# All later conditioning products as two fp16 parts with one constant scale, loaded singly through two buffers, and five raw places for the streamed weights

## The chip, the cores and the metric

The kernel runs on one core of one Trainium2 chip. The metric is the device time of one execution in microseconds. The core has five engines that run side by side: PE (TensorE, the matrix unit), DVE (VectorE), ACT (ScalarE), POOL (GpSimd) and SP (SyncE, which only issues transfers). ACT and POOL can issue transfers too. Each engine and each issuing queue takes its own instructions in a fixed order.

## The reference

One inference step of a one-layer decoder trunk for 288 tokens: a prompt of 256 tokens and 8 sequences of 4 tokens. The model width is 2048. The weights and all inputs are float32.

```python
mod = jax.nn.silu(c) @ P['w_ada'] + P['b_ada']
sh1, sc1, gt1, sh2, sc2, gt2 = [m[:, None, :] for m in jnp.split(mod, 6, axis=-1)]
xn = rmsnorm(x, P['g_norm1']) * (1.0 + sc1) + sh1
mix, st = mixer(xn, states[l], P)
x = x + gt1 * mix
xn = rmsnorm(x, P['g_norm2']) * (1.0 + sc2) + sh2
x = x + gt2 * (jnp.square(jax.nn.relu(xn @ P['w_ff1'])) @ P['w_ff2'])
...
y = rmsnorm(x, g_final)
```

`c` has 9 rows: one for the prompt and one for each of the 8 sequences. So the conditioning product `silu(c) @ w_ada` reads a matrix of 2048 x 12288 for only 9 rows; it gives the shift, scale and gate of both norms. `mixer` multiplies `xn` with `w_in`, runs three branches (a gated linear recurrence, gated linear attention "GLA", and mLSTM with a matrix memory), multiplies each branch with a weight of its own, merges the three products with sigmoid gates, and multiplies with `w_out`. The feed-forward has width 8192. The outputs are `y` and the new states of all branches.

## The kernel before

All activations lie with features on the 128 partitions and the 288 tokens along the row. The kernel holds two versions of the program: a fast one, and a full one in float32 that runs only where a flag, computed at the end of the fast one, says that its scaling was out of range. `fast` in the code tells them apart. Only the fast one runs here.

**Large weights.** `stream` (its matmuls are line 211 of the profile) goes through a block of 512 output columns in granules. For each granule it loads 128 x 1024 float32 values (512 KB) from memory into a raw place, has ACT write the high part (`hi`, scaled by a constant, line 198) and DVE the rest (`lo`, line 134, with a sum of the rest as a mark in the tile `gd`), both fp16, and then has PE do 24 matmuls of 288 columns: hi times x's high part, hi times x's low part, lo times x's high part. A block over 2048 features has 8 granules, one over 1024 has 4. The pairs of parts lie in five buffers. The raw places are three tiles of their own (`raw`) and four quarters of the tile `xl`, used in a ring of seven. From the output projection on, only the three tiles are used.

**Order.** The instructions of SP stay in the order in which the program is traced (`tc.manual_schedule` for SP). Those of the other engines are ordered when the program is built, by priorities and a simulated timeline, and then stay fixed. `Q` is SP's queue, `G` is POOL's, `S` is ACT's. Inside the feed-forward (`in_order`) PE, ACT and DVE keep the traced order too; its matmuls are line 275 and its conversions line 184.

**Stages.** Early blocks (48 granules, while the scale and shift of the first norm are computed), GLA's gate (16), first merge (48), mLSTM input (16), second merge (48), mLSTM output gate (16), third merge (48), output projection (32), feed-forward (252 steps). A merge takes four times 8 granules for a gate and 4 for a branch. The three branches run beside the merges, a step after each granule (`beside`, `run`).

**Conditioning.** The parts of `w_ada` for GT1, SH2, SC2 and GT2 (the gate of the mixer's residual, the second norm's shift and scale, and the gate of the feed-forward's residual) come in 64 units of 1 MB: 16 for GT1 (two halves of 1024 columns each) and eight for each half of the other three (`sj0`, `sj1` for SH2, `sm0`, `sm1` for SC2, `gt0`, `gt1` for GT2). A unit is loaded, held in the list `held`, and later visited: its small matmuls go to one bank `pa`, 32 columns wide, four groups side by side. `every` sets a pattern of letters, and after each granule `run` does the next one: L loads the next unit (`load_one`; the buffer is the next of `slots["ids"]`, the queue is `slots["queue"]`), V visits all units held, F up to four, C does one step of a unit's conversion, E evaluates a result put off, a point does nothing. A load must wait until the last reader of its buffer is done.

Two kinds of units exist before. `cond_product` multiplies the float32 weights directly (line 390). `cond_parts` (line 451), used for `sj1`, `sm1` and `gt1`, first finds a scale for each row from the sum of absolute values (ACT, line 429; DVE, lines 430 to 432), then writes the high part (ACT, line 435) and the rest (DVE, line 437, into every second half word of the raw buffer itself), and scales the 32 columns of `silu(c)`, which lie as three bf16 parts (`silu_parts`), for that row.

From the mLSTM output gate on, the loads go out on SP:

```python
merge(1, ygla, io["wbg"])
slots.update(ids=(None,), n=0, queue=Q)
every("L . . CC CC V" + 12 * " .", skip=10)
...
visit()
slots.update(ids=(None, "st", 5), n=0)
every("L L . L CC CC CC CC CC CC . V . . . L L L CC CC CC CC CC CC V" + 3 * " . . . L L L V", skip=4)
merge(2, yml, io["wbm"])
```

`None` stands for the tile `ag`, which the second merge also uses for its gates; `"st"` for a pair of tiles, and a number for one of ten large tiles.

**Second norm.** After the last output projection block come the residual, the sum of squares, the root (`rstd_of`), `second_norm` and the first feed-forward matmuls. The units of `gt0` are visited in that stretch.

**Check.** `certify` squares the marks in `gd`, sums them over the partitions with one matmul (line 140), and reduces them to one number (lines 139 to 143); it is called twice early in the feed-forward and twice near its end.

Of the kernel before, what the change touches and what calls it, by code (L numbers as in the profile page):

```python
# [8 lines left out]
F32 = mybir.dt.float32  # L9
# [45 lines left out]
def trunk(ctx, tc, io, fast):  # L55
    nc = tc.nc
    R = F16 if fast else F32R
    WS, XS, YS, MS, ZS = (2.0 ** e if fast else 1.0 for e in (14, 6, 5, 4, 4))
# [61 lines left out]
    gd = wp.tile([P, 768], F32, tag="gd", name="gd", bufs=1) if fast else None  # L120
    marks = [0, 544]

    def mark(w=False):

        if not fast:
            return None
        i = 0 if w else 1
        marks[i] += 1
        assert marks[0] <= 544 and marks[1] <= 768
        return gd[:, marks[i] - 1:marks[i]]  # L130
# [5 lines left out]
    def certify(of, a, b, least):  # L136

        sq, p = t288()[:, 0:b - a], misc()[:, 0:b - a]
        V.tensor_tensor(out=sq, in0=gd[:, a:b], in1=gd[:, a:b], op=ALU.mult)
        T.matmul(p, ones, sq, start=True, stop=True)  # L140
        V.tensor_scalar(sq, p, least, None, ALU.is_ge)
        V.scalar_tensor_tensor(sq, p, BIG, sq, ALU.is_le, ALU.mult)
        V.tensor_reduce(out=of, in_=sq, axis=AX.X, op=ALU.min)
# [211 lines left out]
    def raw_tile():  # L355
# [5 lines left out]
        if i in ("xh", "xl"):  # L361
# [47 lines left out]
    high = {"ids": (None,), "n": 0}  # L409

    def high_tile():

        i = high["ids"][high["n"] % len(high["ids"])]
        high["n"] += 1
        if i is None:
            return sp.tile([P, 2048], F16, tag="uh", name=nm("uh"), bufs=3)
        if "xl" not in high:
            high["xl"] = flat(big.tile([P, KT, N], F32, tag="xl", name=nm("xl")))[:, 0:4096].bitcast(F16)
        return high["xl"][:, 2048 * i:2048 * i + 2048]

    def cond_parts(name, load, each, finish):
# [3 lines left out]
        def parts(u, ks):  # L425

            e = [[sc([P, 1], "ue", 12) for _ in range(2)] for _ in u]
            for (w, h, c), (t, scale) in zip(u, e):
                S.activation(h, w, AF.Abs, accum_out=t)
                V.tensor_scalar(t.bitcast(I32), t.bitcast(I32), 0x7F800000, None, ALU.bitwise_and)  # L430
                V.tensor_scalar(t, t, 2.0 ** -86, 2.0 ** -14, ALU.max, ALU.mult)
                V.tensor_scalar(scale.bitcast(I32), t.bitcast(I32), -1, 254 << 23, ALU.mult, ALU.add)
                yield
            for (w, h, c), (t, scale), k in zip(u, e, ks):
                S.activation(h, w, AF.Copy, scale=scale)
                S.activation(c, silp[:, 32 * k:32 * k + 32], AF.Copy, scale=t)
                V.scalar_tensor_tensor(words(w, 0, F16), w, scale, h, ALU.mult, ALU.subtract)  # L437
                yield

        def products(u, q):  # L440
# [3 lines left out]
            for _ in u[1]:  # L444
                pass
            for i, (w, h, c) in enumerate(u[0]):
                a = 0 if each == 2 else 256 * i
                for n, v in enumerate((h, words(w, 0, F16))):
                    v = v.rearrange("p (m j f) -> p j m f", j=4, f=32)
                    for j in range(4):  # L450
                        pace["prod"] = T.matmul(ps[32 * j:32 * j + 32, a:a + 256], c, v[:, j], start=q == i == n == 0,
                                                stop=q == KT // each - 1 and n == 1, skip_group_check=True)

        def end():
            for h in range(3 - each):
                with tc.high_priority():
# [3 lines left out]
                    V.tensor_tensor(out=pv[:, :, 0:9], in0=pv[:, :, 0:9], in1=o, op=ALU.add)  # L460
                    finish(h, pv)

        for q in range(KT // each):
            def ld(q=q):
                raw = raw_tile()
                load(raw, q)
                w = raw if len(raw) == 2 else [raw[0][:, 0:1024], raw[0][:, 1024:2048]]
                h = high_tile()
                u = [(w[i], h[:, 1024 * i:1024 * i + 1024], sp.tile([P, 32], BF16, tag="uc", name=nm("uc"), bufs=6)) for i in range(2)]
                return u, parts(u, [each * q + (i if each == 2 else 0) for i in range(2)])  # L470
# [19 lines left out]
    def ada(kind):  # L490
        def load(raw, k):
# [3 lines left out]
            else:  # L495
                slots["queue"].dma_start(raw[0].rearrange("p (h m) -> p h m", h=2), wada[kind][:, k].rearrange("h p m -> p h m"))
        return cond_product(kind, load, 1, 2048, silu_c, ada_finish(kind))

    def ada_half(name, kind, h, parts=False):
# [6 lines left out]
        if parts:  # L506
# [40 lines left out]
    def units():  # L547
# [8 lines left out]
        for h in range(2):  # L556
            yield from ada_half(f"sj{h}", SH2, h, h == 1)
        for h in range(2):
            yield from ada_half(f"sm{h}", SC2, h, h == 1)
        for h in range(2):  # L560
            yield from ada_half(f"gt{h}", GT2, h, h == 1)
# [15 lines left out]
    def visit(n=99):  # L577

        evaluate()
        for _ in range(min(n, len(held))):  # L580
            name, raw, products, end = held.pop(0)
            products(raw)
            if end:
                done.add(name)
                if name == "gt0":
# [4 lines left out]
    def step(cs):  # L590
        for c in cs:
# [4 lines left out]
            elif c == "C":  # L596
                with tc.issue_after(pace["hi"].ins), tc.issue_after(pace["lo"].ins):
                    next((0 for u in held if len(u[1]) == 2 and next(u[1][1], 1) is None), 0)
# [79 lines left out]
    if fast:  # L678
# [3 lines left out]
        at.update(raw=(None, 0, None, 1, None, 2, 3))  # L682
# [282 lines left out]
    every("")  # L965
    slots.update(queue=G)
# [32 lines left out]
    every("L L L L V . . .")  # L999
    slots.update(ids=(6, 7, "st", None), n=0)  # L1000
# [328 lines left out]
    def merge(br, y, w):  # L1329
        for b in range(4):  # L1330
            if br == 0 and b == 2:
                visit()
                slots.update(ids=(None,), n=0)
                every("L . V . . .", skip=5)
# [12 lines left out]
            if br == 1 and b == 0:  # L1347
                finish(gla_[0])
                slots.update(ids=("st",), n=0)
# [783 lines left out]
```

## Time and profile before

| what | value |
| --- | --- |
| median of 3 runs | 1841.35 us (1841.3 to 1843.49) |
| profiled execution | 1841.84 us, span of its instructions 1840.0 us |
| PE busy | 1778.8 us, 97% of the span |
| DVE, ACT, POOL busy | 1159.8, 931.1, 209.5 us |
| moved by DMA | 422.98 MB, mean 230 GB/s |
| mean granted clock of PE | 0.991 |

The span runs from the first to the last instruction of the program; the rest of the execution's time lies around it. An engine is busy while one of its instructions runs; issuing a transfer or waiting is not counted. In rows of groups stand the line, the engine, the operation, what is written and read, the shapes and the count, then busy time, mean duration in ns, and the idle time of the engine just before these instructions with what ended it. In a timeline a row has its start, its length, and in brackets the idle time ahead of it and what ended that.

### The profile page before, as it was taken

To read this page: it belongs to the slowest core of one execution; us is meant where nothing else is said; L and a number is where in the kernel's file an instruction comes from. 1 tells how busy PE (TensorE), PEld (TensorE's weight loads), DVE (VectorE), ACT (ScalarE), POOL (GpSimd) and SP (SyncE) were. 2 spreads that over 40 slices of the span, in tenths; PEclk is the share of its full clock that TensorE was granted. 3 is DMA by queue.
4 is the path that set the end of the run, shared out by engine and by line. 5 is a ranking of instruction groups with operands and counts; after the bars stand their busy time and mean duration, and the time that the engine had idled before them with its cause. 6 is when DMAs were issued, how large, how long until landed. Compare 5 with 4: busy or idle time off the path is not lost.

```text
span 1840.0 us, 38642 instructions
## 1 busy us (share of the span) xinstructions
PE 1778.8 (97%) x15784; PEld 1380.0 (75%) x15784; DVE 1159.8 (63%) x2575; ACT 931.1 (51%) x1364; POOL 209.5 (11%) x287
## 2 busy tenths in 40 slices
PE   8999999999999999999999999999999999999996
PEld 6787667786777877777767677777777777777775
DVE  4778855646684467886459676556666655555565
ACT  5324475445455354576359465645545544444443
POOL 0002201111142010011002510000000000000261
PEclk9999999999999999999999999999999999999998
DMA  9999756647845469656797775566565555555531
GB/s 394 414 409 355 275 213 246 218 161 286 277 149 173 141 202 316 228 207 251 278 362 293 285 279 170 183 217 206 176 211 186 186 172 183 175 181 180 176 127 54
DMA packets 113451, 422.98 MB, mean 230 GB/s; under 512 B 11808, under 2 KB 12096, under 8 KB 110064
## 3 DMA queue, kind: packets, MB, share of 16 engines
q1 hardware_dynamic: 97040, 361.04, 55.7%
q0 software_dynamic: 11472, 42.79, 6.6%
q10 hardware_dynamic: 4752, 16.60, 2.3%
q8 instruction: 125, 2.05, 0.5%
q14 instruction: 62, 0.51, 0.1%
HBM read 403.56 MB, written 16.81 MB: 228 GB/s over the span
## 4 chain that ended last, share of the span: by engine, by line
PE 56%; DMA 5%; DVE 5%; ACT 2%; issue 2%; SPq 0%; POOL 0%; ACTq 0%; DVEq 0%; POOLq 0%
PE mm L275 32%; PE mm L211 12%; PE pi L275 8%; DMA raw<-wout 2%; DVE pair L134 2%; ACT pair L198 1%; DMA xl<-wbm 1%; PE pa L390 1%; DMA st<-mC 1%; DMA xl<-win 1%; DVE s L437 0%; DMA s<-mC 0%; PE px L1597 0%; DMA o_C_s<-st 0%; PE px L1683 0%
## 5 line engine op out<-in xcount | busy, mean ns | idle before, releaser
L211 PEld LDWEIGHTS <-pair 128*128 128x128 f16 x6528 | 631.3, 98 | 210.1 <-issue 23.2
L275 PEld LDWEIGHTS <-pair 128*128 128x128 f16 x6144 | 601.8, 98 | 159.8 <-issue 5.5
L211 PE MATMUL mm<-x,pair 128*128 128x288 f16 x4320 | 562.0, 288 | 6.6 <-DVE s L769 2.2
L134 DVE SCALAR_TENSOR_TENSOR pair<-xl,pair 128x1024 f16<-128x1024 f32 x229 | 282.9, 1238 | 219.9 <-ACT pair L198 117.0
L134 DVE SCALAR_TENSOR_TENSOR pair<-raw,pair 128x1024 f16<-128x1024 f32 x207 | 255.4, 1235 | 196.6 <-ACT pair L198 116.6
L275 PE MATMUL mm<-hx,pair 128*128 128x288 f16 x2472 | 320.2, 287 | 0.0
L275 PE MATMUL mm<-z,pair 128*128 128x288 f16 x2448 | 313.1, 288 | 4.0 <-ACT z L1854 3.4
L211 PE MATMUL mm<-s,pair 128*128 128x288 f16 x1920 | 245.9, 288 | 11.1 <-ACT ag L1341 3.6
L198 ACT ACTIVATE pair<-xl 128x1024 f16<-128x1024 f32 x137 | 144.0, 1054 | 201.8 <-PE mm L211 121.2
L198 ACT ACTIVATE pair<-raw 128x1024 f16<-128x1024 f32 x135 | 142.0, 1052 | 159.2 <-PE mm L211 77.5
L134 DVE SCALAR_TENSOR_TENSOR pair<-s,pair 128x1024 f16<-128x1024 f32 x92 | 113.8, 1237 | 104.4 <-ACT pair L184 104.4
L184 ACT ACTIVATE pair<-s 128x1024 f16<-128x1024 f32 x92 | 96.9, 1054 | 120.9 <-PE mm L275 99.7
L184 ACT ACTIVATE pair<-xl 128x1024 f16<-128x1024 f32 x92 | 96.8, 1055 | 120.9 <-PE mm L275 94.4
L184 ACT ACTIVATE pair<-raw 128x1024 f16<-128x1024 f32 x72 | 75.7, 1054 | 97.5 <-PE mm L275 70.6
L1879 POOL TENSOR_SCALAR s<-s,mod 128x256 f32<-128x256 f32 x16 | 14.7, 921 | 665.1 <-DVE s L1895 665.1
L275 PE MATMUL pi<-hx,pair 128*128 128x288 f16 x600 | 89.9, 287 | 0.0
L275 PE MATMUL pi<-z,pair 128*128 128x288 f16 x624 | 85.6, 288 | 0.0
L211 PE MATMUL px<-x,pair 128*128 128x288 f16 x288 | 41.8, 287 | 3.4 <-DVE pair L134 2.8
L1364 POOL TENSOR_TENSOR s<-s,t 128x288 f32<-128x288 f32 x16 | 20.0, 1279 | 162.7 <-DVE t L1363 130.9
L390 PE MATMUL pa<-s,silc 128*32 128x128 f32 (+2 forms) x768 | 33.0, 320 | 1.7 <-DVE silc L317 1.2
L134 DVE SCALAR_TENSOR_TENSOR hx<-t,hx 128x288 f16<-128x288 f32 x64 | 29.3, 458 | 6.7
L1873 DVE TENSOR_TENSOR t<-t 128x288 f32<-128x288 f32 x64 | 29.2, 456 | 3.0
(494 smaller groups left out, 1544.3 us busy)
## 6 DMA issues: line engine op xcount, KB each, us to landing
xl<-win SPq DMA_DIRECT2D x109, 512.0 KB, 5.5
s<-wf SPq DMA_DIRECT2D x92, 512.0 KB, 3.4
xl<-wf SPq DMA_DIRECT2D x92, 512.0 KB, 3.5
raw<-win SPq DMA_DIRECT2D x83, 512.0 KB, 6.1
raw<-wf SPq DMA_DIRECT2D x72, 512.0 KB, 3.4
s<-wq SPq DMA_DIRECT2D x20, 1024.0 KB, 13.0
raw<-wout SPq DMA_DIRECT2D x32, 512.0 KB, 6.5
s<-wada SPq DMA_DIRECT2D x13, 1024.0 KB, 8.3
```

The costliest lines, as they stand in the source:

```text
L134: return V.scalar_tensor_tensor(dst, src, scale, hi if fast else hi.bitcast(F32), op, ALU.subtract, accum_out=mark(w))
L184: pace["hi"] = S.activation(hi, raw, AF.Copy, scale=WS)
L198: pace["hi"] = S.activation(hi, raw, AF.Copy, scale=WS)
L211: pace["last"] = T.matmul(ps, w[:, kk, ms], x, start=k == k0 and i == 0, stop=k == kt - 1 and i == 2)
L275: pace["last"] = T.matmul(self.ps[m][:, :N], a[:, kk, m * P:(m + 1) * P], x, start=k == 0 and i == 0, stop=k == 4 * self.kg - 1 and i == 2)
L390: pace["prod"] = T.matmul(ps[32 * j:32 * j + 32, h * w // 4:(h + 1) * w // 4], stat(k), v[:, j], start=k == 0 and h == 0, stop=k == kt - 1 ...
L1364: (V if br == 1 else G).tensor_tensor(out=a, in0=a, in1=t, op=ALU.add)
L1873: V.tensor_tensor(out=q, in0=r, in1=r, op=ALU.mult)
L1879: G.tensor_scalar(a[:, 0:NP], a[:, 0:NP], mod[:, GT2, k, 0:1], None, ALU.mult)
```

## The change

In the fast version:

- Every unit of GT1, SH2, SC2 and GT2 becomes `cond_parts`. The scale is now the constant 2^16 (`AS`): ACT writes the high part, DVE the rest with a mark, and the columns of `silu(c)` are used unscaled. A conversion step is now one half of a unit (one ACT and one DVE instruction). The result is multiplied by 1/`AS`, one more small DVE instruction for each half.
- C goes to the first unit held that has a step left; a unit is only begun while fewer than three are converted and not yet visited (`ready_`). The letter v visits one unit.
- The ring of raw places has five members from the start to the end of the output projection: the three tiles and the lower two quarters of `xl`. The upper half of `xl` (`"x"`) becomes a buffer for conditioning units, and `ag` the second one. In the second merge only `"x"` is used; in the output projection `"st"` and tile 9 are added.
- The patterns are new for every stage. The norm stretch now visits two units ahead of the sum and the rest behind it; no result is put off.
- `silu_parts` moves from the second merge to the end of the early blocks.
- `gd` grows to 1024 marks, and `certify` works in pieces of at most 256 columns.
- In the feed-forward the raw places are two quarters of tile 8, two of `xl`, two of tile 3 and the three tiles (nine instead of eleven).

The diff, cut:

```diff
-    marks = [0, 544]
+    marks = [0, 704]
...
+        if i == "x":
+            return [extra["xl"][:, 2048:4096]]
...
-        def parts(u, ks):
-            e = [[sc([P, 1], "ue", 12) for _ in range(2)] for _ in u]
-            for (w, h, c), (t, scale) in zip(u, e):
-                S.activation(h, w, AF.Abs, accum_out=t)
-                V.tensor_scalar(t.bitcast(I32), t.bitcast(I32), 0x7F800000, None, ALU.bitwise_and)
...
-            for (w, h, c), (t, scale), k in zip(u, e, ks):
-                S.activation(h, w, AF.Copy, scale=scale)
-                S.activation(c, silp[:, 32 * k:32 * k + 32], AF.Copy, scale=t)
-                V.scalar_tensor_tensor(words(w, 0, F16), w, scale, h, ALU.mult, ALU.subtract)
-                yield
+        def parts(u):
+            ready_[0] += 1
+            t = sp.tile([P, 2048], F16, tag="uh", name=nm("uh"), bufs=3)
+            for i, w in enumerate(u["w"]):
+                h = t[:, 1024 * i:1024 * i + 1024]
+                S.activation(h, w, AF.Copy, scale=AS)
+                rest(words(w, 0, F16), w, AS, h, w=True)
+                u["h"].append(h)
+                yield
...
+                    for u in held if fast else ():
+                        if (u[1]["h"] or ready_[0] < 3) and next(u[1]["parts"], 1) is None:
+                            break
-            elif c in "VF":
+            elif c in "VFv":
                 with tc.high_priority(), tc.issue_after(pace["last"].ins):
-                    visit(4 if c == "F" else 99)
+                    visit({"V": 99, "F": 4, "v": 1}[c])
...
-        at.update(raw=(None, 0, None, 1, None, 2, 3))
+        at.update(raw=(None, 0, None, 1, None))
...
-    every("L L L L V . . .")
-    slots.update(ids=(6, 7, "st", None), n=0)
+    if fast:
+        every("L . . . . . . . L C C v . . L .")
+        slots.update(ids=("x", None), n=0)
...
     run(stream(win, B_GATE, act1, KT, gate_silu(0)))
...
-    slots.update(ids=(None, 7), n=0)
-    every("L L V . . .")
+    if fast:
+        every("C C v L")
...
     merge(0, ylru, io["wbl"])
...
         run(stream(win, B_MX + b, act1, KT, to_slot(mx, 4 * b)))
     visit()
     every("")
+    if fast:
+        slots.update(ids=("x",), n=0)
+        every("L . . C C v")
...
     merge(1, ygla, io["wbg"])
-    slots.update(ids=(None,), n=0, queue=Q)
-    every("L . . CC CC V" + 12 * " .", skip=10)
+    if fast:
+        visit()
+        slots.update(ids=("x", None), n=0, queue=Q)
+        step("L")
+        every("L C C v")
...
-    visit()
-    slots.update(ids=(None, "st", 5), n=0)
-    every("L L . L CC CC CC CC CC CC . V . . . L L L CC CC CC CC CC CC V" + 3 * " . . . L L L V", skip=4)
+    if fast:
+        every("L C C v")
     merge(2, yml, io["wbm"])
...
+    if fast:
+        visit()
+        slots.update(ids=("x", None, "st", 9), n=0)
+        every("L L . . " + 5 * "C C v L " + "L L . . CC CC . .")
...
-                    visit(4)
+                    visit(2 if fast else 4)
...
+    if fast:
+        slots.update(ids=("x", None), n=0)
+        every("L . . . . . C . C . . v", skip=8)
...
     run(feed_forward())
```

The patterns stand, from the top, ahead of GLA's gate, the first merge, the second merge (its pattern set behind the mLSTM input), the output gate, the third merge, the output projection and the feed-forward.

More of the change, by code (lines that the diff above doesn't have):

```diff
@@ L57, in trunk @@
     R = F16 if fast else F32R
-    WS, XS, YS, MS, ZS = (2.0 ** e if fast else 1.0 for e in (14, 6, 5, 4, 4))
+    WS, XS, YS, MS, ZS, AS = (2.0 ** e if fast else 1.0 for e in (14, 6, 5, 4, 4, 16))
     PSUM = bass.MemoryType.PSUM
@@ L128, in mark @@
         marks[i] += 1
-        assert marks[0] <= 544 and marks[1] <= 768
+        assert marks[0] <= 704 and marks[1] <= 1024
         return gd[:, marks[i] - 1:marks[i]]
@@ L134, in rest, with certify @@
         return V.scalar_tensor_tensor(dst, src, scale, hi if fast else hi.bitcast(F32), op, ALU.subtract, accum_out=mark(w))
[L136 to L143, printed above, removed]
+    oks = []
+    def certify(a, b, least):
+        for a in range(a, b, 256):
+            n = min(b - a, 256)
+            sq, p, of = t288()[:, 0:n], misc()[:, 0:n], okc[:, len(oks):len(oks) + 1]
+            V.tensor_tensor(out=sq, in0=gd[:, a:a + n], in1=gd[:, a:a + n], op=ALU.mult)
+            T.matmul(p, ones, sq, start=True, stop=True)
+            V.tensor_scalar(sq, p, least, None, ALU.is_ge)
+            V.scalar_tensor_tensor(sq, p, BIG, sq, ALU.is_le, ALU.mult)
+            V.tensor_reduce(out=of, in_=sq, axis=AX.X, op=ALU.min)
+            oks.append(of)
     def t288(dt=F32):
@@ L443, in products @@
             ps = acc_[0]
-            for _ in u[1]:
+            for _ in u["parts"]:
                 pass
-            for i, (w, h, c) in enumerate(u[0]):
-                a = 0 if each == 2 else 256 * i
+            ready_[0] -= 1
+            for i, (w, h) in enumerate(zip(u["w"], u["h"])):
+                k, a = each * q + (i if each == 2 else 0), 0 if each == 2 else 256 * i
                 for n, v in enumerate((h, words(w, 0, F16))):
@@ L466, in ld @@
                 load(raw, q)
[L467 to L470, printed above, removed]
+                u = {"w": raw if len(raw) == 2 else [raw[0][:, 0:1024], raw[0][:, 1024:2048]], "h": []}
+                u["parts"] = parts(u)
+                return u
             yield name, ld, lambda u, q=q: products(u, q), end if q == KT // each - 1 else None
@@ L556, in units @@
         for h in range(2):
-            yield from ada_half(f"sj{h}", SH2, h, h == 1)
+            yield from ada_half(f"sj{h}", SH2, h)
         for h in range(2):
-            yield from ada_half(f"sm{h}", SC2, h, h == 1)
+            yield from ada_half(f"sm{h}", SC2, h)
         for h in range(2):
-            yield from ada_half(f"gt{h}", GT2, h, h == 1)
+            yield from ada_half(f"gt{h}", GT2, h)
     left = units()
@@ L584, in visit @@
                 done.add(name)
-                if name == "gt0":
+                if name == "gt0" and not fast:
                     late.append(end)
@@ L1331, in merge @@
             if br == 0 and b == 2:
-                visit()
-                slots.update(ids=(None,), n=0)
-                every("L . V . . .", skip=5)
+                if fast:
+                    pass
+                else:
+                    visit()
+                    slots.update(ids=(None,), n=0)
+                    every("L . V . . .", skip=5)
             if br == 0:
@@ L1348, in merge @@
                 finish(gla_[0])
-                slots.update(ids=("st",), n=0)
-                silu_parts()
-                every("L . V . L . V . . . L . . CC CC V" + 40 * " .")
+                if fast:
+                    pass
+                else:
+                    slots.update(ids=("st",), n=0)
+                    every("L . V . L . V . . . L . . CC CC V" + 40 * " .")
             if br == 2 and b == 0:
@@ L1370, in merge @@
             run(stream(w, b, lambda k: (y[0][:, k, :], y[1][:, k, :]), 8, ev))
-    slots.update(ids=(None, 7), n=0)
-    every("L L V . . .")
+    if fast:
+        every("C C v L")
+    else:
+        slots.update(ids=(None, 7), n=0)
+        every("L L V . . .")
     merge(0, ylru, io["wbl"])
@@ L1767, in trunk @@
     merge(1, ygla, io["wbg"])
-    slots.update(ids=(None,), n=0, queue=Q)
-    every("L . . CC CC V" + 12 * " .", skip=10)
+    if fast:
+        visit()
+        slots.update(ids=("x", None), n=0, queue=Q)
+        step("L")
+        every("L C C v")
+    else:
+        slots.update(ids=(None,), n=0, queue=Q)
+        every("L . . CC CC V" + 12 * " .", skip=10)
     mo = slot(3)
```

68 lines of the change are left out of this document (35 added, 33 removed).

## The prediction

> **What bounds the kernel now.** I read the page's first part, then its slices, then windows cut at the stages, then the engines' timelines around the visits to the conditioning units, and last the waits of SP.
>
> ```profile
> span 1840.0 us, 38642 instructions
> PE 1778.8 (97%) x15784; PEld 1380.0 (75%) x15784; DVE 1159.8 (63%) x2575; ACT 931.1 (51%) x1364; POOL 209.5 (11%) x287
> PEclk9999999999999999999999999999999999999998
> ...
> GB/s 394 414 409 355 275 213 246 218 161 286 277 149 173 141 202 316 228 207 251 278 362 293 285 279 170 183 217 206 176 211 186 186 172 183 175 181 180 176 127 54
> ...
> L134 DVE SCALAR_TENSOR_TENSOR pair<-xl,pair 128x1024 f16<-128x1024 f32 x229 | 282.9, 1238 | 219.9 <-ACT pair L198 117.0 <-ACT pair L184 102.2
> L198 ACT ACTIVATE pair<-xl 128x1024 f16<-128x1024 f32 x137 | 144.0, 1054 | 201.8 <-PE mm L211 121.2 <-DMA xl<-win 41.9 <-issue 19.5
> ```
>
> PE is busy 97% of the span and everything else waits for it: even ACT's idle time before a conversion is mostly ended by PE (121.2 of 201.8 us). So a gain has to shorten PE's own list or close one of its gaps, and a loss opens a gap. The profiled execution took 1841.84 us, 1.84 more than its span and 0.5 above the median 1841.35; the sum below starts from 1841.84.
>
> ```profile
> 710.00:775.00 65.00, 60.63 (x547) 45.37 (x546) 48.68 (x125) 29.92 (x48) 4.24 (x8) 0.97 0.79 268
> 775.00:934.00 159.00, 155.14 (x1401) 120.07 (x1402) 99.30 (x205) 90.06 (x133) 16.57 (x13) 1.00 0.67 259
> 934.00:1042.00 108.00, 101.97 (x924) 77.35 (x920) 81.91 (x186) 76.28 (x114) 33.27 (x30) 1.00 0.84 314
> 1042.00:1054.00 12.00, 8.89 (x135) 5.01 (x129) 9.10 (x28) 6.50 (x12) 5.58 (x6) 1.00 0.48 167
> ```
>
> Columns: length, then PE, weight loads, DVE, ACT, POOL, clock, DMA share, GB/s. These are the mLSTM output gate, the third merge, the output projection and the second norm: PE lacks 4.4, 3.9, 6.0 and 3.1 us.
>
> **What the change does, part by part.** A granule is 24 matmuls of 288 columns. Unit numbers count from GT1's first.
>
> *Matmuls of the conditioning.* 40 units (GT1, half of SH2, SC2 and GT2) go from float32 to two fp16 parts.
>
> ```profile
> 200.00:1041.00 841.00, 32.31 (x400) 11.55 (x400) 0.99 0.67 238
> 1041.00:1054.00 13.00, 7.32 (x128) 3.95 (x128) 1.00 0.44 154
> ...
> 200.00:1041.00 841.00, 8.85 (x256) 6.25 (x256) 0.99 0.67 238
> 1041.00:1840.00 799.00, 4.07 (x128) 3.08 (x128) 0.99 0.55 181
> ```
>
> The first two rows are line 390 alone (float32), the others line 451 (parts); PE's busy time comes first. Up to 1041 us, 32 float32 units cost 32.31 us (1.01 each) and 16 units in parts 8.85 (0.55 each). After the change 49 units lie there, all in parts: 49 x 0.55 = 27 against 41.2, so **-14**. In the feed-forward 11 units come singly instead of 8 in three lots: 11 x 0.55 - 4.07, **+2.0**.
>
> *Conversions.* A unit in parts costs ACT two passes of 1.05 us and DVE two of about 1.43 (below). 40 units newly pay that; 24 lose their Abs, their exponent steps and their scaled columns. For DVE that is some +100 us over 1000 us with about a third idle. PE hides it except where DVE is already full:
>
> ```profile
> L437 DVE SCALAR_TENSOR_TENSOR s<-s,ue,uh 128x1024 f16<-128x1024 f32 x14 | 19.8, 1425 | 0.5 <-ACT uh L435 0.5
> ...
> 541.00:545.00 4.00, 0.88 (x8) 0.56 (x6) 4.00 (x6) 1.55 (x2) 4.00 (x4) 1.00 0.47 162
> 545.00:549.00 4.00, 3.55 (x16) 2.27 (x16) 3.72 (x7) 2.24 (x6) 3.71 (x4) 0.59 0.53 168
> ```
>
> There unit 18 is flushed and one DVE pass can land in the queue ahead of the pass that PE waits for: between 0 and 10 us over the mixers, nearest to one or two passes: **+2.5**.
>
> *Certify.* 53 units leave 106 more marks in the first check, 22 in the second; pieces of at most 256 make three pieces of two, twice.
>
> ```profile
> 1109.42 0.73 PE L140 MATMUL px<-t,ones 128*128 128x273 f32 x2 [0.60 <-DVE t L139]
> 1111.76 0.43 PE L140 MATMUL px<-t,ones 128*128 128x58 f32 x2 [1.62 <-DVE t L139]
> ```
>
> PE's order is fixed there, so it stands between pieces: 2.34 us after one of 273 columns. The new ones, of 123 and 22 columns, cost less, since the DVE passes between them shrink: I estimate 1.7 and 1.3 (ends 1 and 2.3 each), **+3.0**.
>
> *Output projection.* It keeps five raw places instead of three and gets one load every four granules. PE's idle time there:
>
> ```profile
> L211 PE MATMUL mm<-s,pair 128*128 128x288 f16 x311 | 40.2, 287 | 5.9 <-DVE rs_t L1802 2.5 <-DVE pair L134 1.7 <-ACT pair L198 0.9
> ```
>
> That is 946 to 994 us; with five places I take it as gone, **-5.9** (ends 0 and -6). *Second norm:* the float32 units there (7.32 us) fill a gap that the chain of the norm sets, so making them cheap earns nothing, and two units' parts, up to four DVE passes of 1.43, now fall into that chain: 0 to +5.7, taken **+2**. *Five places instead of seven* earlier: the early blocks run at the DMA's limit (394 to 414 GB/s in the first slices) whatever the depth: 0 to +4, **+1**.
>
> So far 1841.84 - 14 + 2.0 + 2.5 + 3.0 - 5.9 + 2 + 1 = **1832.4**.
>
> *The loads in the output gate and the third merge.* There the loads go out on SP, which runs in the order of the program, with the weights behind them. The change loads unit 27 ahead and then repeats "L C C v". Two buffers are both taken, so each L reuses the buffer that the v just ahead of it frees: v after granule 3, granule 4's weights, L, granule 5's weights. SP can't issue granule 5's weights before PE has finished that v, when PE has one granule left. Before, three empty steps stood between V and L, and the trace shows what that was worth:
>
> ```profile
> 809.39 0.33 SPq L197 DMA_DIRECT2D raw<-win  x1
> 828.26 0.38 SPq L505 DMA_DIRECT2D ag<-wada  x1
> 828.73 0.42 SPq L197 DMA_DIRECT2D xl<-wbm  x1
> ...
> SPq L505 <- PE pa L451: 18.7, 1, 18.7
> ...
> 827.59 0.29 PE L451 MATMUL pa<-uh,uc 128*32 128x256 f16 x4
> ...
> 829.03 11.94 PE L211 MATMUL mm<-x,pair 128*128 128x288 f16 x96
> 840.80 4.45 PE L211 MATMUL mm<-s,pair 128*128 128x288 f16 x35
> ...
> 834.76 1.06 ACT L198 ACTIVATE pair<-xl 128x1024 f16<-128x1024 f32 x1 [8.95 <-DMA xl<-wbm]
> 835.85 1.23 DVE L134 SCALAR_TENSOR_TENSOR pair<-xl,pair 128x1024 f16<-128x1024 f32 x1 [8.35 <-ACT pair L198]
> ```
>
> SP stood 18.7 us at the load until the visit of 827.59 freed its buffer; the next weights went out at 828.73, were converted from 834.76, and their pair was whole at 837.08. PE lived on the 96 matmuls (four granules, 11.94 us) in hand, to 840.97: 3.9 us to spare. With one granule it runs dry at 829.03 + 2.98 = 832.0 and waits **5.1 us**. That visit held three units; counted from SP's release, a single one ends near 828.05, and the wait is 837.08 - 831.0 = **6.0**. I take 5.6.
>
> How often: L at steps 4, 8, 12 of the gate's 16 granules, at 0, 4 ... 44 of the merge's 48, and once at the start of the output projection, whose first load wants the buffer of the unit flushed just before: 16 x 5.6 = 90. Unit 27's own load stands ahead of the gate's first weights, with no granule in hand: 8.6. Together **+98**. mLSTM's steps in the gate cover some of it, but its state transfers fill the DMA there (share 0.79 in the row above) and make the weights later: I set one against the other. Of the old gaps in these stages (4.4 and 3.9) most fall into the new waits: **-7**.
>
> Each wait also slows the clock:
>
> ```profile
> 722.00:726.00 4.00, 1.24 (x32) 0.84 (x34) 0.79 (x4) 3.31 (x7) 0.00 (x0) 1.00 1.01 364
> 726.00:730.00 4.00, 4.00 (x25) 2.68 (x18) 3.50 (x10) 0.00 (x0) 0.86 (x2) 0.58 0.91 230
> ```
>
> A gap of about 2.8 us is followed by 4 us at 0.58, that is 1.7 lost; the gap of 541 to 545 likewise (0.59). 17 x 1.7 = 29, of which I take **+26**. Sum: 1832.4 + 98 - 7 + 26 = 1949.4, say **1950**.
>
> In the Trainium skill, "DMA: Bandwidth & Descriptors", section "Issuing engines are not separate DMA queues", transfers from SP, ACT and POOL share the same 16 engines, and issuing from several engines saves only the sequencer's time, usually small. By that rule alone it would not matter that these loads stand in SP's order, and the sum would end at 1832.4, the first rival's time. The row of 18.7 us speaks against it here: the sequencer's time is the wait that stands in it.
>
> **Rivals.**
> A, faster: the loads don't hold the weights, because a buffer is free earlier than I read or enough weights stand ahead. Place: SP between v and L. For it: merges before lost little beside such loads (3.9 us in 159). Against it: they had four granules in hand. Time 1832.4; it ends below before only if each of the 17 loads costs PE less than 9.4 / 17 = 0.55 us; dearer mixers or norm bring it to 1842. Chance 0.12, of which 0.03 within 0.2%.
> B: the waits are there and the clock holds: 1950 - 26 = 1924. Against it, both rows after a gap. 0.18.
> C: the visit's DVE pass is late, so PE runs granule 4 ahead of the visit and has nothing after it: 16 x 2.98 more, 1998. For it: DVE is busy 99 of 159 us there. 0.15.
> Forecast, 0.55: 1950, by itself 1915 to 1985.
>
> **Numbers.** The range leaves out A and little above C's lower part: 1900 to 1995. A tenth of a per cent is the spread of the runs shown, so 0.2% (3.7 us) is about what tells a change from none: faster 0.09, same 0.03, slower 0.88.
>
> **What would show it.** Right: the gate and the merge stretch from 224 us to some 330; SP's waits for the parts' matmuls grow from single cases to one per load; ACT's conversions there wait for DMA of weights; PE's timeline shows about 24 matmuls, a gap of 5 to 6 us, then 72; the granted clock dips in each. Wrong: SP issues weights while a load's buffer is held, or PE keeps four granules in hand. Then look whether the single visits take 0.55 us, whether the idle time in the output projection is gone, and whether PE stands longer at the checks and in the norm.

## The result, and the profile after

The changed kernel takes 1969.93 us (median of 4 runs, 1964.57 to 1973.52), the kernel before 1842.24 (the three runs above and a fourth, 1841.3 to 1843.49): 1.069 times as long, 95% interval 1.0664 to 1.0717. It is slower by some 128 us; forecast were 1950 (1900 to 1995). The profiled execution took 1973.52 us, a span of 1971.7. First the top of its page, and from the page's groups of instructions the stream's matmuls with x:

```profile
span 1971.7 us, 38868 instructions
PE 1818.5 (92%) x15900; PEld 1398.3 (71%) x15900; DVE 1240.6 (63%) x2665; ACT 942.0 (48%) x1300; POOL 199.0 (10%) x284
PEclk8999999999999988988888989999999999999998
...
L216 PE MATMUL mm<-x,pair 128*128 128x288 f16 x4320 | 587.8, 295 | 70.1 <-ACT pair L203 61.6
```

PE falls from 97% to 92% of the span, and its idle time is ended by ACT's conversions of weights (line 203). The clock line shows where: most of the eights lie between 0.35 and 0.6 of the span. The next view is windows of after (length, PE, weight loads, DVE, ACT, POOL, clock, DMA share, GB/s): from 720 us to the end of the output gate, then the third merge, the output projection and the norm.

```profile
720.00:820.20 100.20, 72.88 (x650) 51.62 (x652) 58.68 (x138) 36.16 (x55) 4.41 (x8) 0.85 0.69 255
820.20:1056.60 236.40, 183.26 (x1402) 130.42 (x1391) 116.25 (x225) 91.11 (x116) 13.74 (x16) 0.86 0.42 162
1056.60:1161.20 104.60, 96.90 (x832) 74.97 (x830) 73.55 (x146) 53.28 (x62) 29.93 (x27) 0.97 0.73 274
1161.20:1176.70 15.50, 6.57 (x74) 3.46 (x72) 10.69 (x27) 8.93 (x14) 6.12 (x5) 0.69 0.88 352
```

The third merge took 162 us before with PE idle for 3.9; now it takes 236 with PE idle for 53, while the DMA is at 0.42. Neither PE nor the DMA is full there, so the time is not lost for want of either; the timeline below shows what each waits for. The lengths of all stages, each from the last evacuation or matmul of one stage to that of the next (e6 is the run of that name below):

| stage (us) | before | after | e6 |
| --- | --- | --- | --- |
| to the end of the attention's gate | 273.7 | 273.9 | 274.1 |
| first merge, to its last gate | 169.8 | 166.7 | 166.7 |
| mLSTM input, to the second merge's first gate | 102.8 | 112.6 | 111.6 |
| second merge, to its last gate | 151.0 | 155.2 | 155.9 |
| its end and the output gate | 79.1 | 111.8 | 79.3 |
| third merge | 162.0 | 236.4 | 163.5 |
| output projection | 103.2 | 104.6 | 93.5 |
| norm | 12.3 | 15.5 | 11.6 |
| feed-forward, and after it | 786.2 | 795.0 | 793.7 |

Of 131.7 us between the profiled executions, 107 lie in two stages. One turn of the loop there, in the timeline of after (start, length, in brackets the idle time ahead and its end; SP's rows are issues of transfers):

```profile
898.29 0.28 PE L445 MATMUL pa<-ag,silp 128*32 128x256 f16 x4
898.51 3.11 PE L216 MATMUL mm<-x,pair 128*128 128x288 f16 x24
898.62 0.38 SPq L501 DMA_DIRECT2D ag<-wada  x1
899.05 1.81 SPq L202 DMA_DIRECT2D raw<-win  x1
...
901.91 0.38 SPq L202 DMA_DIRECT2D xl<-wbm  x1
...
905.30 1.06 ACT L203 ACTIVATE pair<-raw 128x1024 f16<-128x1024 f32 x1 [13.08 <-DMA raw<-win]
...
906.41 11.27 PE L216 MATMUL mm<-x,pair 128*128 128x288 f16 x72 [4.79 <-ACT pair L203]
...
917.61 0.29 PE L445 MATMUL pa<-uh,silp 128*32 128x256 f16 x4
...
918.28 0.38 SPq L501 DMA_DIRECT2D xl<-wada  x1
```

The visit ends at 898.5; within 0.1 us SP issues the load that wanted its buffer, and 0.4 us later the next weights. PE has 24 matmuls in hand, one granule, and stands 4.79 us until those weights have landed (by 905.3) and are converted. Then come 72 matmuls and the next visit. There are 17 such gaps: 8.7 at the first load, 7.3, 5.8 and 4.3 in the output gate, twelve of 4.6 on average in the third merge, 7.9 at the start of the output projection; 88.9 us together. (These are counted from the start of one matmul to the start of the next, less the 0.12 us that one takes at the full clock. The idle time that the rows show is some 0.16 shorter for each: 4.4 on average in the third merge, 86.3 together.) Behind each gap the clock falls; windows of the same turn:

```profile
901.00:905.00 4.00, 0.62 (x6) 0.26 (x3) 0.00 (x0) 0.00 (x0) 0.00 (x0) 0.91 1.02 414
905.00:907.00 2.00, 0.59 (x3) 0.42 (x4) 0.61 (x1) 1.70 (x2) 0.00 (x0) 0.50 1.03 422
907.00:909.00 2.00, 2.00 (x10) 1.24 (x9) 2.00 (x5) 2.00 (x3) 0.00 (x0) 0.50 0.45 180
909.00:911.00 2.00, 2.00 (x10) 1.27 (x9) 2.00 (x3) 2.00 (x3) 0.00 (x0) 0.50 0.00 0
911.00:914.00 3.00, 3.00 (x26) 2.38 (x25) 2.57 (x6) 0.09 (x1) 0.00 (x0) 0.98 0.00 0
```

Ten matmuls in 2 us at 0.50 against 26 in 3 us at 0.98. Counted over the output gate, the third merge and the start of the output projection, matmuls that take about 240 ns and not 122.5 lose 35.5 us, against 1.0 in the same stages before.

### The profile page after: what moved, and what is told of

It reads as the page before. It is cut to its first block, busy times and chain, and to the rows that moved or that the text cites. A ratio compares the mean times of both kernels' runs of the same rounds, so it can differ in the third digit from the quotient of the medians.

```text
span 1971.7 us, 38868 instructions
## 1 busy us (share of the span) xinstructions
PE 1818.5 (92%) x15900; PEld 1398.3 (71%) x15900; DVE 1240.6 (63%) x2665; ACT 942.0 (48%) x1300; POOL 199.0 (10%) x284
## 4 chain that ended last, share of the span: by engine, by line
PE 75%; DMA 11%; DVE 5%; issue 4%; ACT 3%; POOL 1%; SPq 0%; ACTq 0%; DVEq 0%; POOLq 0%
PE mm L280 30%; PE mm L216 30%; PE pi L280 8%; DMA raw<-win 3%; DMA xl<-win 3%; DMA xl<-wada 2%; DVE pair L134 2%; PE pa L445 1%; ACT pair L203 1%; PE pa L397 1%; PE px L216 1%; DMA raw<-wout 1%; DMA xl<-wbm 1%; DMA raw<-wbm 1%; DMA ag<-wada 0%
## 5 line engine op out<-in xcount | busy, mean ns | idle before, releaser
L216 PE MATMUL mm<-x,pair 128*128 128x288 f16 x4320 | 587.8, 295 | 70.1 <-ACT pair L203 61.6
L134 DVE SCALAR_TENSOR_TENSOR pair<-raw,pair 128x1024 f16<-128x1024 f32 x250 | 308.1, 1235 | 246.3 <-ACT pair L203 149.0
L134 DVE SCALAR_TENSOR_TENSOR pair<-xl,pair 128x1024 f16<-128x1024 f32 x165 | 204.0, 1237 | 153.5 <-ACT pair L203 90.6
L216 PE MATMUL mm<-s,pair 128*128 128x288 f16 x1920 | 261.6, 299 | 31.2 <-ACT pair L203 25.5
L203 ACT ACTIVATE pair<-raw 128x1024 f16<-128x1024 f32 x163 | 170.6, 1050 | 206.7 <-DMA raw<-win 100.1
L134 DVE SCALAR_TENSOR_TENSOR pair<-s,pair 128x1024 f16<-128x1024 f32 x113 | 140.0, 1240 | 125.6 <-ACT pair L189 125.4
L203 ACT ACTIVATE pair<-xl 128x1024 f16<-128x1024 f32 x109 | 114.6, 1051 | 134.2 <-DMA xl<-win 60.6
L189 ACT ACTIVATE pair<-raw 128x1024 f16<-128x1024 f32 x87 | 91.4, 1054 | 124.1 <-PE mm L280 84.4
L134 DVE SCALAR_TENSOR_TENSOR xl<-xl,uh 128x1024 f16<-128x1024 f32 x72 | 97.7, 1371 | 26.0 <-ACT uh L428 26.0
L189 ACT ACTIVATE pair<-xl 128x1024 f16<-128x1024 f32 x56 | 58.8, 1054 | 80.2 <-PE mm L280 69.2
L428 ACT ACTIVATE uh<-xl 128x1024 f16<-128x1024 f32 x72 | 73.8, 1044 | 34.3 <-DMA xl<-wada 34.3
L280 PE MATMUL pi<-z,pair 128*128 128x288 f16 x624 | 86.3, 289 | 0.0
L134 DVE SCALAR_TENSOR_TENSOR ag<-ag,uh 128x1024 f16<-128x1024 f32 x48 | 64.8, 1353 | 10.4 <-ACT uh L428 10.3
L428 ACT ACTIVATE uh<-ag 128x1024 f16<-128x1024 f32 x48 | 49.8, 1043 | 21.2 <-DMA ag<-wada 21.2
```

Of the source, the lines that this page charges most:

```text
L134: return V.scalar_tensor_tensor(dst, src, scale, hi if fast else hi.bitcast(F32), op, ALU.subtract, accum_out=mark(w))
L189: pace["hi"] = S.activation(hi, raw, AF.Copy, scale=WS)
L203: pace["hi"] = S.activation(hi, raw, AF.Copy, scale=WS)
L216: pace["last"] = T.matmul(ps, w[:, kk, ms], x, start=k == k0 and i == 0, stop=k == kt - 1 and i == 2)
L280: pace["last"] = T.matmul(self.ps[m][:, :N], a[:, kk, m * P:(m + 1) * P], x, start=k == 0 and i == 0, stop=k == 4 * self.kg - 1 and i == 2)
L428: S.activation(h, w, AF.Copy, scale=AS)
```

## The experiments

The theory: a load on SP whose buffer is freed late in the program's order stops the weights behind it, and what it costs depends on the number of granules between the visit that frees the buffer and the load (the distance): the fewer, the more. After has distance 1. Rival 1: the extra megabyte ahead of the weights takes bandwidth. Rival 2: the conversions of 40 more units hold up ACT and DVE. The first five runs change only the patterns of the output gate and the third merge (e8 also loads one unit more ahead), or the queue of their loads.

**e1, distance 3** (`-every("L C C v")` / `+every("C C L v")`, twice).

> The same loads, buffers and queue as after, but in the output gate and the third merge the load comes three steps behind the visit that frees its buffer (C C L v) and not one (L C C v). Theory (a load blocked on SP holds the weights of the next granules back): the wait in each loop was 4.6 us with one granule in hand; two more granules are worth 5.96 us, so it goes to 0. The 15 loop gaps (72.8 us) and their half-clock windows (about 2.0 us each, 30 us) go, the first load's gap (8.7) and the one at the start of the output projection (7.9) stay: 1970 - 103 = 1867 us (1855 to 1885). Rival 1 (the megabyte ahead of the weights takes the DMA's bandwidth, whoever waits): the same megabytes in the same queue, so near 1970, not under 1945. Rival 2 (the added conversions on ACT and DVE hold the weights' conversions): unchanged, 1965 to 1975.

Measured 1876.17 us (1875.28 to 1883.8), 9 above the mark. The loop's gaps are gone but for short ones; in the output gate three, of 1.0 to 1.7 us idle and 4.2 together, are left, which DVE and ACT end with other work than weights.

**e2, distance 2** (`+every("C L C v")`, twice).

> As the first run, but the load two steps behind the visit (C L C v). Theory: each loop's wait is 4.6 - 2.98 = 1.6 us, so 15 x 3 = 45 us of gaps go, and of the half-clock windows about half: 1910 us (1895 to 1930). Rival 1 (bandwidth): near 1970. Rival 2 (conversions): near 1970.

Measured 1905.82 us (1901.39 to 1914.19), 4 from the mark.

**e3, meant as distance 0** (`+every("C C vL .")`, twice).

> As the first run, but the load in the same step as the visit, right behind it (C C vL .), so that no granule is in hand when the visit ends. Theory: each loop's wait grows by one granule, 4.6 + 2.98 = 7.6 us; 15 x 3 = 45 us more: 2015 us (2000 to 2030). Rival 1 (bandwidth): near 1970. Rival 2 (conversions): near 1970.

Measured 1868.47 us (1864.71 to 1873.13) where 2015 was expected. The mistake was in the edit. With v ahead of L only one unit is held, so the load takes the other buffer, the one visited a period earlier: distance 4. SP's issues in e3's third merge, and SP's waits at the loads in e3 (total us, times, longest):

```profile
881.69 0.38 SPq L501 DMA_DIRECT2D xl<-wada  x1
882.16 0.42 SPq L202 DMA_DIRECT2D raw<-win  x1
882.67 0.38 SPq L202 DMA_DIRECT2D raw<-wbm  x1
883.15 0.53 SPq L202 DMA_DIRECT2D xl<-wbm  x1
883.77 0.39 SPq L202 DMA_DIRECT2D raw<-wbm  x1
894.11 0.38 SPq L501 DMA_DIRECT2D ag<-wada  x1
```

```profile
SPq L501 <- PE pa L445: 173.9, 19, 13.5
```

Here too SP stands at the loads until PE's visit, 9 us on average, and the weights go out behind it in one burst every 12.4 us; yet PE no longer waits, since it has four granules in hand while SP stands. A long wait on a queue is no cost by itself; what counts is what is in hand behind it.

**e8, really distance 0** (e3 with `+step("LL")` for `step("L")`, so that two units are held).

> As the third run, but two units are loaded ahead, so that each load of C C vL . now does want the buffer of the visit just ahead of it: no granule in hand. (In the third run I had miscounted: with one unit held, the load took the other buffer, free for four granules, and nothing waited.) Theory: each loop waits 4.6 + 2.98 = 7.6 us, 15 x 3 = 45 us more than after, and a few more at the start, where the second load waits for the last gate of the second merge: 2017 us (2000 to 2035). Rival (the place of the load in the order of the step decides, not the age of its buffer): as the third run, 1868.

Measured 2020.46 us (2 runs), 3 from the mark. The same group of PE's matmuls in e8, after, e2, e1 and e3, in this order (idle time ahead, and what ended it):

```profile
L216 PE MATMUL mm<-x,pair 128*128 128x288 f16 x4320 | 590.3, 296 | 112.6 <-ACT pair L203 103.2 <-ACT x L741 4.1 <-DVE pair L134 1.5
```

```profile
L216 PE MATMUL mm<-x,pair 128*128 128x288 f16 x4320 | 587.8, 295 | 70.1 <-ACT pair L203 61.6 <-ACT x L741 3.5 <-DVE pair L134 2.2
```

```profile
L216 PE MATMUL mm<-x,pair 128*128 128x288 f16 x4320 | 573.4, 290 | 36.0 <-ACT pair L203 25.4 <-ACT x L741 3.3 <-DVE pair L134 2.2
```

```profile
L216 PE MATMUL mm<-x,pair 128*128 128x288 f16 x4320 | 563.9, 288 | 20.2 <-ACT pair L203 8.4 <-ACT x L741 3.4 <-ACT s L1795 2.8
```

```profile
L216 PE MATMUL mm<-x,pair 128*128 128x288 f16 x4320 | 565.7, 288 | 16.3 <-ACT pair L203 8.0 <-ACT x L741 4.4 <-DVE pair L134 1.5
```

103.2, 61.6, 25.4, 8.4, 8.0 stand there for ACT's conversions at distance 0, 1, 2, 3 and 4. The stream's matmuls with s, the branches, add 22.5, 25.5, 15.4, 7.2 and 7.5. So the time that PE waits for converted weights is 125.7, 87.1, 40.8, 15.6 and 15.5 us: it falls by some 40 us for each of the first two granules and by 25 for the third, until the loop has nothing left to give (the 15.5 are the first load and the start of the output projection). In the third merge the gap of a turn is 7.6 us at distance 0, 4.6 at 1, between 1.0 and 2.9 at 2, and at 3 all but two, of about 1 us, are gone: about one granule of 2.98 us a step. Rivals 1 and 2 forecast no change in any of these runs and fall; the megabytes and the conversions are the same in all of them. How much the megabyte ahead of the weights delays them within one wait was not tested.

**e4, the loads on POOL's queue** (`-queue=Q` / `+queue=G`, back to Q for the output projection).

> The pattern L C C v and the two buffers of after, but the loads of the output gate and the third merge are issued by POOL instead of SP. Theory: POOL stands at the load, SP goes on with the weights; the gaps of the loop and of the first load go (81 us and some 32 of half clock): 1857 us (1845 to 1880), the upper end if POOL's additions of the third merge, which stand behind the waiting load, come late and hold DVE. Rival 1 (bandwidth): the same megabytes start at the same moment, near 1970. Rival 2 (conversions): near 1970.

Measured 1875.8 us (1874.16 to 1879.45), at the upper end expected. With the pattern of after and distance 1, the loop's gaps go as soon as the load stands on another queue than the weights: of the 87 us that PE waits for converted weights in after, 7.5 are left, at the start of the output projection. Besides these, PE now waits once for 6.8 us in the output gate, for DVE's work on the branch there. This run alone tells waiting in the queue from the distance as such.

**e12, the same in the kernel before** (third merge, four times: `-V . . . L L L` / `+V L L L . . .`).

> The kernel before with one thing moved: in the third merge the three empty steps stand behind the loads and not between the visit and the loads (V L L L . . . for V . . . L L L), four times. Nothing else of the change is in it. Theory: the first load of each three waits for the visit one granule ahead and holds the weights: a gap of some 5.1 us and 2.0 of half clock, four times, 28 us: 1843 + 28 = 1871 us (1861 to 1880). Rival (what costs in after is not the distance but the single visits and their conversions): within 5 us of before.

Measured 1869.09 us (1868.36 to 1869.68), 27.4 more than before (1841.66 in the same comparison; ratio 1.0149, 1.0132 to 1.0166). Nothing of the new fp16 units, the constant scale, the five raw places or the single visits is in it. One of its gaps:

```profile
876.02 0.38 SPq L505 DMA_DIRECT2D ag<-wada  x1
876.45 1.43 SPq L197 DMA_DIRECT2D xl<-win  x1
876.79 3.11 PE L211 MATMUL mm<-x,pair 128*128 128x288 f16 x24
...
884.21 2.10 PE L211 MATMUL mm<-x,pair 128*128 128x288 f16 x8 [4.30 <-ACT pair L198]
```

The matmuls with x in the third merge, of before and of e12:

```profile
L211 PE MATMUL mm<-x,pair 128*128 128x288 f16 x768 | 96.2, 287 | 0.4 <-DVE t L1363 0.4
```

```profile
L211 PE MATMUL mm<-x,pair 128*128 128x288 f16 x768 | 102.5, 294 | 11.6 <-ACT pair L198 11.2
```

The mechanism is there, but the sum fits better than its parts. PE is idle for 3.5, 4.3, 2.7 and 1.4 us behind the four visits, 11.9 together, where the theory had four times 5.1. The third merge grows from 162.0 to 186.0 us: PE's idle time there from 3.9 to 18.4, and half clock takes some 5 us more; the rest was not traced.

**e5, the two starts** (e3, and `-step("L")`; output projection `-ids=("x", None, "st", 9)` / `+ids=("st", "x", 9, None)`).

> As the third run (C C vL .), but without the load ahead of the output gate, and the output projection takes its buffers in the order st, x, 9, ag, so that its first load wants a buffer that has long been free. Theory: the two waits that the third run keeps (8.1 us at the start of the output gate, 7.7 at the start of the output projection) come from a load on SP whose buffer was flushed just before; both go, with about 4 us of half clock: 1868 - 20 = 1848 us (1843 to 1855). Rival (the two waits belong to the change of stage, whatever is loaded): 1865 to 1870.

Measured 1855.24 us (1853.61 to 1861.42): 13 us less than e3, not 20. Both waits are gone: the stage with the output gate goes from 87.0 to 76.1 us, the output projection from 105.3 to 95.9; the third merge grew from 155.9 to 161.1. What took 5 us there was not found.

**e6, the norm** (e5, and `-visit()`, `+every(7 * "C C vL . " + "C C v . ")` in the output projection).

> As e5_starts, but the loop goes on through the output projection with no flush ahead of it (7 times C C vL ., then C C v), so that every unit is converted and visited before the second norm. Theory (two units' conversions, two passes of ACT and two of DVE, stand in the chain of the norm): the stretch from the last matmul of the output projection to the first of the feed-forward goes from 15.3 to about 12 us, the total from e5_starts by 3 us: 1845 us (1840 to 1851). Rival (the norm got longer because the float32 matmuls of before no longer fill it, or for its own reasons): the stretch stays at 15 us and the total at that of e5_starts.

Measured 1852.25 us (1846.76 to 1858.04), above the range expected. The 3 us less than e5 are there, but the runs spread by more, so the stretch itself has to show the effect. The norm, in windows of e6 behind its output projection, and what stood in it in the timeline of after:

```profile
951.10:1044.60 93.50, 93.50 (x850) 72.48 (x849) 70.10 (x143) 48.79 (x57) 31.48 (x27) 1.00 0.67 239
1044.60:1056.20 11.60, 3.56 (x9) 2.00 (x8) 5.19 (x18) 4.81 (x10) 5.42 (x6) 0.64 0.83 316
```

```profile
1165.50 1.99 ACT L428 ACTIVATE uh<-xl 128x1024 f16<-128x1024 f32 x2
...
1168.08 1.52 DVE L134 SCALAR_TENSOR_TENSOR xl<-xl,uh 128x1024 f16<-128x1024 f32 x1
...
1169.61 1.47 DVE L134 SCALAR_TENSOR_TENSOR xl<-xl,uh 128x1024 f16<-128x1024 f32 x1
...
1170.98 0.46 DVE L624 TENSOR_TENSOR t<-t,t 128x288 f32<-128x288 f32 x1
1171.49 2.29 PE L626 MATMUL pi<-t,ones 128*128 128x288 f32 x4 [3.39 <-DVE t L624]
```

One unit's passes stood in the chain: the sum of squares (line 624) waited behind two DVE passes of 1.5 us. Without them the stretch is 11.6 us in e6, less than the 12.3 of before although no conditioning matmul fills it. The output projection now has PE busy for all of its 93.5 us.

**e7, the first merge's loads on SP** (e6, and `+slots.update(queue=Q); every("C C vL .")` for `every("C C v L")`).

> As e6_norm, but the loads of the first merge and the mLSTM input go out on SP with the pattern C C vL . instead of on POOL with C C v L. Theory (the wait of 4.8 us at 452 us comes from a conversion that stands in ACT's and DVE's order ahead of the transpose that PE needs and waits for a load that POOL issued late): the load comes in time, the gap and some 2 us of half clock go: 1838 us (1833 to 1846), at or under before. Rival (the loads on SP hold the weights of the first merge): 5 to 40 us longer than e6_norm. Rival (the gap belongs to the gated linear attention itself): as e6_norm.

Measured 1855.52 us (1853.38 to 1858.2), 3 more than e6 where 14 less were expected. Half right in the stages: the one with the mLSTM input goes from 111.6 to 107.3 us, but the first merge goes from 166.7 to 175.2, where PE now stands 3.7 us for the attention's state from memory and the rest is spread.

**e9, later conversions in the second merge** (e6, and `-every("L . . C C v")` / `+every("L . . . . C C v")`; output projection in threes).

> As e6_norm, but in the second merge the conversion begins five granules behind its load and not three (L . . . . C C v, six units instead of eight); the output projection makes up for them with a loop of three granules (C C vL). Theory (ACT stands 25.9 us at eight conversions there for loads that land late, with the last gate evacuations behind it, and PE then waits): ACT's waits at these conversions fall under 5 us, the three later blocks of the second merge go from 155.9 to about 151 us: 1847.5 us (1843 to 1852). Rival (the wait is for the evacuations' own work on ACT): the same time as e6_norm, 1852.

Measured 1854.56 us (1851.75 to 1855.79). The theory fell: the second merge got longer (162.7 us against 155.9 in e6), and ACT's waits stayed. The timeline of e9 shows what one of them waits for:

```profile
548.47 6.95 POOL L1486 TENSOR_TENSOR s<-bdw,con 128x128 f32<-128x128 f32 x8 [0.29 <-DVE bdw L1484]
555.36 0.74 POOL L501 DMA_DIRECT2D xl<-wada  x1
...
562.69 2.00 ACT L428 ACTIVATE uh<-xl 128x1024 f16<-128x1024 f32 x2 [6.74 <-DMA xl<-wada]
```

POOL issues the load only when its own work of 13.6 us (two such rows) is done; it lands at 562.7, and ACT stands in front of the conversion with everything behind it. How many granules the program puts between load and conversion doesn't help when the issuer is late. Why the merge got longer than in e6 is not shown.

**e10, those loads on SP around the mLSTM input** (e9, and from the first merge's last block `+slots.update(queue=Q); every("C C v . " + 6 * "C C vL . ")`).

> As e9_later_parts, but from the last block of the first merge to the end of the mLSTM input the loads go out on SP (C C v . once, then C C vL .) and no longer on POOL, where they stand behind a load of the attention's state that waits for PE 11.7 us. Theory: the conversion at 452 us finds its data, the gap of 3.7 to 4.8 us and its half clock go, the stretch with the mLSTM input and the first block of the second merge goes from 111.6 to about 107 us: 1843 us (1838 to 1849). Rival (the DMA is full there, share 1.0, so that the megabyte comes late from any queue, or the state of the attention comes late instead): no shorter than e9_later_parts.

Measured 1852.26 us (1849.79 to 1855.97) where 1843 was expected. For the stage at hand the theory holds; windows of it in e9 and in e10:

```profile
440.70:549.10 108.40, 100.31 (x913) 74.41 (x910) 91.27 (x193) 66.87 (x97) 24.83 (x39) 1.00 0.69 243
```

```profile
441.50:546.30 104.80, 100.94 (x919) 74.99 (x916) 92.17 (x193) 66.37 (x97) 23.03 (x36) 1.00 0.68 242
```

104.8 us are 2.0 more than before. The lengths alone would prove little, since the same stage took 114.7 us in the one trace of e11, whose code there is that of e9. But no conversion of a unit between 441 and 545 us waits for its load any more, and the gap of PE behind the conversion at 452 us, 3.5 us in e6, is gone. The total moved by 2.3 us, less than the spread of the runs. The conversion at 561 us, whose load is still on POOL, now holds ACT for 10.5 us; whether that took the gain back is not shown.

**e11, pieces of 288** (e9, and `-range(a, b, 256)` / `+range(a, b, 288)`).

> As e9_later_parts, but the check takes its marks in pieces of at most 288 columns and not 256: four pieces instead of six. Theory (PE stands between the pieces): 1.3 us less at each of the two calls, and some half clock: 2 to 4 us less than e9_later_parts, near 1845. Rival (the time at the check is one chain whatever its pieces): the same as e9_later_parts.

Measured 1852.23 us (1849.49 to 1858.7), which doesn't tell it from e9. The edit saves one piece, not two (371 marks still make two), so about 1.2 us was to be had.

None of these versions beats the kernel before. The nearest is e6, at 1.0048 times before (1.0032 to 1.0064). What it still loses is 13.7 us in the mLSTM input and the second merge and 7.5 in the feed-forward and behind it; it gains 9.7 in the output projection and 3.1 in the first merge.

## Why the prediction was right

The mechanism is the one forecast, place for place: gate and third merge take 107 us more, by the table of stages (241 to 348; 224 to some 330 were forecast, between marks inside the two stages), PE's timeline shows 24 matmuls, a gap, then 72, and ACT waits for weights from memory. Rival A (the loads don't hold the weights) is excluded by e1, e2, e8 and e4, rival C (a granule run ahead of the visit, nothing behind it) by the 24 matmuls behind each of the 16 visits, rival B (the clock holds) by the 0.50 in the windows. The Trainium skill, "DMA: Bandwidth & Descriptors", section "Issuing engines are not separate DMA queues", says that issuing from several engines saves only the sequencer's time to initiate a transfer, which is usually small. Here the other queue was worth 94 us between after and e4: what it saved was not that time but a wait in the queue, behind which the weights stood.

The terms of the sum, forecast and measured:

| term | forecast | measured | where from |
| --- | --- | --- | --- |
| matmuls of the conditioning, to the norm | -14 | -8.1 | 41.16 to 33.07, rows below |
| single units in the feed-forward | +2.0 | +2.8 | 4.07 to 6.86 |
| conversions in the mixers | +2.5 | +14 | the two stages with the mLSTM input and the second merge, 0.7 of the first row in them |
| check in pieces | +3.0 | +2.8 | first to last piece: 2.34 to 3.95 us, and 2.29 to 3.48 |
| output projection without its first load | -5.9 | -7.8 | 104.6 - 7.9 - 1.3 (half clock) against 103.2 |
| norm | +2 | +3.2 | 12.3 to 15.5 |
| five raw places early | +1 | under 0.5 | 273.7 to 273.9 |
| loop, 17 loads | +98 | +88.9 | the gaps above |
| old gaps there | -7 | -7.7 | 9.4 to 1.7 |
| half clock there | +26 | +34.5 | 1.0 to 35.5 |

The rows come from the profiled executions. Without what stands in two rows they add up to some 122 of the 131.7 us between these. Most of the rest is the attention's gate, where PE's idle time from 192 us on grows from 3.5 to 7.2 us (and takes back what the cheaper matmuls saved there), and half clock in the feed-forward, which grows from some 3 to 6 us. The row of line 445 alone in windows of after (up to the norm, norm, feed-forward):

```profile
200.00:1161.00 961.00, 33.07 (x784) 17.09 (x784) 0.94 0.58 209
1161.00:1177.00 16.00, 2.96 (x64) 1.81 (x64) 0.69 0.86 346
1177.00:1972.00 795.00, 6.86 (x176) 3.64 (x176) 0.99 0.53 178
```

The forecast is 20 us short of the median. Four terms were mis-sized. A unit up to the norm costs 0.67 us (33.07 / 49) and not 0.55, which was the price of units most of which were visited three or four at a time. The conversions in the mixers cost more than five times what was put down. I sized them by DVE's full queue; in the stage with the mLSTM input (9.8 of the 14 us) they cost by standing in ACT's order ahead of other work while their load is late, as the wait of 7.1 us at 452 us and the 4.6 us of PE behind it show; in e10, where that wait is gone, the stage is down to 104.8 us. What the 4.2 us of the second merge are was not found. The loop's wait is 4.6 us and not 5.6: I had PE wait for the whole pair, DVE's rest included (to 837.08 in the prediction), while it goes on as soon as ACT has written the high part, which was there 1.26 us earlier (834.76 + 1.06); in the timeline of after ACT is done at 906.36 and PE starts at 906.41. And the half clock costs 2.0 us for each gap (34.5 / 17), where I had taken 1.5. These last two errors, 9.1 too much and 8.5 too little, nearly cancel: that the loop's part of the sum came out so close, 117 forecast and 115.7 measured, is partly luck. The gains that were forecast came: the output projection had no more idle time once its first load was out of the way, which e6 shows at 93.5 us against 103.2.

## What to carry to other kernels

On a queue that keeps the program's order, count for every load how many tiles of the consumer lie between the instruction that frees its buffer and the load, and compare that number with what the transfer and the conversion behind it take: here 7.4 us (899.05 to 906.41 in the timeline above), so three granules of 2.98. Read this from the order of the queue, not from the length of its waits: in e3 SP stands 9 us at every load for nothing, while in after, with one granule in hand, 4.6 of the 16 us that it stands at a load (902.3 to 918.3 in the timeline above) are lost. A load that shares a queue with an engine's own work can be late by that work, as in e9, and a conversion that waits for it in a fixed order makes what stands behind it late.

## What was not expected of the hardware

Half clock takes nearly the same behind gaps of two lengths: 25.9 us in the third merge with twelve gaps of 4.6 us (after), 24.3 with twelve of 7.6 (e8). The clock records of the traces show it in stretches of 3.41 or 6.83 us there in after and of 6.83 or 10.24 in e8; part of each stretch lies in the gap itself, where PE loses nothing by it. And shorter gaps than I had counted with bring it on, though not each time. At the check of the fast version's marks PE waits twice within 2.4 us, for 0.6 and 1.6 us, in before and in e12 alike; windows behind it, of before and of e12:

```profile
1114.00:1116.00 2.00, 2.00 (x11) 1.25 (x10) 0.47 (x5) 0.00 (x0) 0.00 (x0) 0.56 0.45 119
```

```profile
1142.00:1144.00 2.00, 2.00 (x19) 1.59 (x17) 0.98 (x5) 0.32 (x1) 0.00 (x0) 1.00 0.24 41
```

The same code of the check got 0.56 in one execution and 1.00 in the other. The Trainium skill, "TensorE: Matmul & The Clock Gate", section "HAM oscillation — how this bites in real kernels", gives the rule of no idle gaps of PE above about 3.4 us; before's row shows that two shorter ones, 2.3 us from start to start, can do it.
